# Low parts of two weight pieces by halves, low parts of probabilities in their usual place, both halves of one spectrum cast together

## The chip, the cores and the metric

The kernel runs on one core of a Trainium2 chip. It uses the core's engines side by side: TensorE for matmuls (PE in the profile, its weight loads PEld), VectorE (DVE), ScalarE (ACT), GpSimd (POOL), and SyncE (SP), which here only issues DMAs. Each engine works through its own queue in order; semaphores order the engines among each other. The metric is the time of one execution in device microseconds (us), as the median of several runs.

## The reference, cut to what matters

A trunk of two layers runs over a prompt of 2048 tokens and a sample of 512 tokens, 1024 channels wide, all in float32. Layer 0 is windowed attention, layer 1 Fourier mixing; each is gated, projected and added to its input.

```python
def attention_layer(x, g, w_in, w_out, sink, rel_bias):
    h = rmsnorm(x, g)
    z = h @ w_in                      # 1024 -> q 1024, k 256, v 256, gate 1024
    ...
    o = banded_gqa_with_sink(q, k, v, rel_bias, sink)   # 16 heads, 4 kv heads, |i-j| <= 128
    return x + (o * jax.nn.silu(gate)) @ w_out

def fourier_layer(x, g, w_gate, w_out):
    h = rmsnorm(x, g)
    hg = h.astype(jnp.float32).reshape(b, s, N_FGROUPS, FGROUP_CH)
    f = jnp.fft.fftn(hg, axes=(1, 3), norm="ortho").real
    gate = h @ w_gate
    return x + (f.reshape(b, s, d) * jax.nn.silu(gate)) @ w_out
...
    return rmsnorm(x, final_norm)
```

In the attention, each block of 128 queries meets three blocks of keys; scores get a bias, are exponentiated with their maximum (or the sink) taken off, divided by their sum, and multiplied with the values.

## The kernel before, in words

**Two parts for every operand.** A float32 operand of a matmul is split into a high part (a cast to the type `fp32r`, mostly on ACT) and a low part (the operand minus its high part, on DVE or POOL). A product is then three matmuls: high by high, high by low, low by high (`matmul3`, line 134, and `beside`, line 524).

**Chunks and periods.** The attention phase goes over five chunks of 512 tokens (`CHUNKS`); chunk 0 is the sample, chunks 1 to 4 the prompt. Within a chunk, 19 periods `n` are laid out. Two periods make a pair of heads `p`, one for each two of the chunk's four query blocks. A period also holds a quarter of the projections for the next heads (q and gate weights, tiles `wq`, `wg`, products in PSUM `pj`).

**The order in a period** is written out by hand: `FIRST` for chunk 0, `PERIOD` for the others, as pairs of a step's name and how many periods it lags. The steps that matter here, with their lines:

- `S1`, `S2`: scores on PE (line 661, into `spt`); `b..`: bias and maximum on DVE (line 680); `e..`: exponentials on ACT (line 688); `r..`: reciprocals on DVE (line 694); `m..`: division by the sum, on DVE (line 707 in chunk 0) or ACT (line 701).
- `T0`, `T1`: probabilities transposed on PE into `tp` (line 720); `hi0`, `hi1`: their high parts on ACT (line 733); `lo0`, `lo1`: their low parts on DVE (line 737), both into the tile `pts`.
- `AV1`, `AV2`: probabilities by values on PE (line 780, into `av`); `t2`, `add`: the two halves of that summed (ACT line 800, DVE line 810) into `o`; `mul`, `sp`, `lop`: gate (POOL line 816), high part (ACT line 821), low part (POOL line 825), into `uT`.
- `qH`, `qL`: the next heads' q split (ACT line 584, DVE line 585, tile `qab`), and beside them pieces of the keys (tile `kwin`; ACT line 398, DVE line 403). `W`, `WL`: the next weights split (ACT line 177, POOL line 182, four pieces of 256 columns) and stored to DRAM (POOL line 184) for the later chunks.
- `side`: in chunk 0 alone, at the end of periods 1 to 5, the late weight pieces.

`seq` chains the recorded order on PE, ACT and DVE. On POOL, `pieces` (line 962) is tied only to the last `lop`; the rest of POOL's order is what the scheduler makes of the operands.

**Late weight pieces.** The key weights (pieces 8 and 9, `LATE`) are used in chunk 0 before there is time to store their split form. So chunk 0 fetches each again later (`late_w`): `w32late` is loaded in period 1 or 3; in period 2 or 4 ACT casts the high part (`latehi`, line 1165), POOL forms the low part in four pieces of 256 columns (`latelo`, line 962), and POOL issues two DMAs that store both (line 1168). Line 1198 moves the step `lo1` ahead of `b2a` in periods 3 and 5 of chunk 0, the periods behind a late piece.

**Position transforms.** In the Fourier phase, `position` multiplies a spectrum, split by `halves_of` into high and low parts for each half of its 1024 columns (tile `gp`, ACT line 1713, DVE line 1714), with tables. `step` (line 1989) splits the first half of its first position ahead of time, and leaves the second half to `position`.

Of the kernel before, what the change touches and what calls it, by code (L numbers as in the profile page):

```python
# [14 lines left out]
ALU = mybir.AluOpType  # L15
# [17 lines left out]
LATE = (8, 9)  # L33
# [17 lines left out]
def f32(ap):  # L51
    return ap.bitcast(F32)
# [3 lines left out]
def encoder(  # L56
# [3 lines left out]
    PE, ACT, DVE, POOL, SP = nc.tensor, nc.scalar, nc.vector, nc.gpsimd, nc.sync  # L60
# [26 lines left out]
    wsd = [dram.tile([P, 2, D], F32R, name=f"wsd{i}") for i in range(28)]  # L87
# [50 lines left out]
    def fetch_w(n, name, late=None):  # L138

        w32 = stage[late is not None or n > 19 or n in (6, 7, 18, 19)](f"w32{name}")  # L140
        load = SP.dma_start(w32, w_in[n] if n < 20 else w_out[(n - 20) // 4, (n - 20) % 4])
        if late:
            after(load, late)
        last_fetch[0] = load
        return w32
# [44 lines left out]
    def after(ins, anchor):  # L190

        if anchor is not None:
            tc.add_manual_dep(ins.ins, anchor.ins.name, ISSUE, reason="issue order")
# [10 lines left out]
    def attention_phase():  # L204

        with ExitStack() as es:
# [750 lines left out]
            def pieces(out, a, b, op, n=2):  # L957

                for i in range(n):
                    cs = slice(i * 256, i * 256 + 256)  # L960

                    after(POOL.tensor_tensor(out[:, cs], a[:, cs], b[:, cs], op), last_lo[0])
# [129 lines left out]
            for c in range(len(CHUNKS)):  # L1092
# [67 lines left out]
                def late_w(i):  # L1160
                    w32 = fetch_w(LATE[i], f"late{i}", last_exp[0])

                    def split():
                        hi, lo = (xtile([P, D], F32R, f"late{part}{i}") for part in ("hi", "lo"))
                        seq(ACT, ACT.copy(hi, w32))
                        pieces(lo, w32, f32(hi), ALU.subtract, 4)
                        for part, t in enumerate((hi, lo)):
                            POOL.dma_start(f32(wsd[LATE[i]][:, part]), f32(t))

                    return split  # L1170

                def side(n):
                    if n in (1, 3):
                        side_steps.append(late_w(n // 2))
                    elif n in (2, 4):
                        side_steps.pop()()
                    if k_splits:
                        k_lows.append(k_splits.pop(0)())

                side_steps, k_lows = [], []  # L1180
                low_q, high_q, low_w = [], [], []
                for n in range(19):
# [12 lines left out]
                    order = [a for a in (PERIOD if c else FIRST) if n < 15 or a[0] not in ("hi0", "lo0")]  # L1195
                    if n == 1 and c:
                        order.sort(key=lambda a: a[0] == "qL")
                    if n in (3, 5) and not c:
                        low = order.index(("lo1", 1))
                        order.insert(order.index(("b2a", 0)), order.pop(low))  # L1200
                    if n >= 15:
                        for name, behind in (("hi0", ("T0",)), ("lo0", ("m2a", "m2b"))):
                            at_ = max(i for i, a in enumerate(order) if a[0] in behind)
# [47 lines left out]
    def fourier_phase(tail):  # L1251
        with ExitStack() as es:
# [300 lines left out]
            order = [[16, 17, 18, 19]] + [[a, a + 4, a + 8, a + 12] for a in range(4)]  # L1553
# [147 lines left out]
            def position_loads(name, tab, tiles):  # L1701
                return [gated(name, r, xtile) for r in tiles], table(name, tab, left)

            def halves_of(name, gr, gs, hf, after_one=None):

                out = []
                for i, g in enumerate((gr, gs)):
                    if i and after_one:
                        after_one()
                    if g is not None:  # L1710
                        t = main.tile([P, 2, 512], F32R, align_bytes=LINE, tag="hT", bufs=8, name=f"g{name}_{hf}_{i}")
                        gv = g[hf] if isinstance(g, list) else g[:, hf * 512 : hf * 512 + 512]
                        ACT.copy(t[:, 0], gv)
                        low = DVE.tensor_tensor(t[:, 1], gv, f32(t[:, 0]), ALU.subtract)
                        if chain.get("steps"):
                            seq("dve", low)
                        out.append(t)
                return out
# [98 lines left out]
            class Outs:  # L1817
# [53 lines left out]
                def rest(self):  # L1871
                    self.halve(3)
                    self.own(1, 1)
# [115 lines left out]
            def step(n, *positions):  # L1989
                new, held = [], []  # L1990
                for i, p in enumerate(positions):
                    held.append((position_loads(p[0], p[1], p[4]), None if i else [halves_of(p[0], p[2], p[3], 0), None]))

                def within():
                    for p, h in zip(positions, held):
                        new.extend(position(*p, *h))

                if not n:
                    within()
                end = finish(*pend.pop(0), None, within, n)  # L2000
                chain["turns"] = end
                new = turned(new)
                for f in pend:
                    finish(*f)
                pend[:] = new
# [82 lines left out]
            for i, l in enumerate((w0, w2)):  # L2088
                for a in range(3):
                    t = zt(f"ev{a}_{i}")  # L2090
# [34 lines left out]
            for a in range(4):  # L2125
                for i, l in enumerate((pc, qs)):
# [3 lines left out]
                    t = zt(f"od{a}_{i}")  # L2130
# [205 lines left out]
```

## Time and profile before

| | |
|---|---|
| median of 3 runs | 1536.61 us (1535.53 to 1537.4) |
| the profiled execution | 1536.59 us |
| its span in the profile | 1534.5 us |
| PE busy | 1519.9 us, 99% of the span |
| PE weight loads busy | 1340.0 us, 87% |
| DVE busy | 1119.7 us, 73% |
| ACT busy | 890.4 us, 58% |
| POOL busy | 453.1 us, 30% |
| low parts of the late pieces, L962 `latelo` | 8 instructions of 727 to 756 ns, 63.3 to 83.6 us after the start |
| casts of the spectrum at position 2, L1713 `gp<-g2r`, `g2s` | 4 instructions of 603 to 617 ns, 1355.2 to 1361.3 us after the start |

In rows of the timeline the first number is the start after the span's begin, the second the length, both in us; then engine, line, operation, output `<-` inputs, shapes, and how many instructions were merged into the row. In brackets stands how long the engine was idle before it, and what ended that. A DMA row of POOL is the issue, not the transfer. Records of matmuls overlap, since matmuls are pipelined.

### The profile page before, as it was taken

The numbers are of one execution on the slowest core, as the hardware profiler recorded it, in microseconds if no ns is written. First come the engines' busy times: TensorE is split into PE (matmuls) and PEld (weight loads), VectorE is DVE, ScalarE is ACT, GpSimd is POOL, SyncE is SP. The second block draws the span as 40 slices with busy tenths as digits, with TensorE's granted clock in tenths as the row PEclk, the third lists the DMA queues.
The fourth block names the chain that finished last, engine by engine and source line by source line (L and its number), as shares of the span: only waits on it lengthen the run. The fifth ranks groups of instructions, "written<-read, shape, count | busy, mean of one in ns | idle before, by whom it ended". The sixth has DMA issues, their size and how long they took to land.

```text
span 1534.5 us, 33665 instructions
## 1 busy us (share of the span) xinstructions
PE 1519.9 (99%) x13150; PEld 1340.0 (87%) x13150; DVE 1119.7 (73%) x2431; ACT 890.4 (58%) x1925; POOL 453.1 (30%) x616
## 2 busy tenths in 40 slices
PE   9999999999999999999999999999999999999998
PEld 7999889999898888999988899888888888888886
DVE  5898665777638776468764577667888878888896
ACT  6788634787237884268862577646655654343343
POOL 2576652422414323315124142222212111011100
PEclk9999999999999999999999999999999999999999
DMA  8687687685857766867649666584657679557852
GB/s 322 224 301 247 232 335 280 220 301 174 321 192 244 242 222 231 304 211 228 227 166 379 231 214 233 207 299 163 240 206 249 210 243 413 174 180 278 299 182 91
DMA packets 100731, 372.71 MB, mean 243 GB/s; under 512 B 11236, under 2 KB 22252, under 8 KB 83421
## 3 DMA queue, kind: packets, MB, share of 16 engines
q1 hardware_dynamic: 82716, 297.38, 56.1%
q0 software_dynamic: 16688, 70.04, 11.7%
q10 hardware_dynamic: 1168, 3.15, 0.6%
q8 instruction: 103, 1.69, 0.4%
q14 instruction: 56, 0.45, 0.1%
HBM read 280.06 MB, written 90.47 MB: 241 GB/s over the span
## 4 chain that ended last, share of the span: by engine, by line
PE 88%; DVE 7%; issue 2%; ACT 2%; DMA 1%; POOL 0%; POOLq 0%; ACTq 0%; DVEq 0%; SPq 0%
PE pj L524 27%; PE W L134 6%; PE pj L134 6%; PE tp L134 5%; PE av L780 5%; PE spt L661 5%; PE av L134 5%; PE spt L134 4%; PE tp L720 3%; PE Wo L134 3%; PE Z L134 3%; PE fo L134 2%; PE z L1420 2%; PE Zo L134 2%; PE X L134 2%
## 5 line engine op out<-in xcount | busy, mean ns | idle before, releaser
L524 PE MATMUL pj<-h,wg 64*128 64x512 f32 x1920 | 437.7, 389 | 0.0
L524 PE MATMUL pj<-h,wq 64*128 64x512 f32 x1560 | 379.1, 389 | 0.0
L524 PEld LDWEIGHTS pj<-h,wg 64*128 64x128 f32 x1920 | 332.2, 185 | 17.7
L524 PEld LDWEIGHTS pj<-h,wq 64*128 64x128 f32 x1560 | 285.0, 185 | 12.7 <-DVE q L580 0.2
L680 DVE CUSTOM_DVE_ANT_0 S<-spt,b 128x385 f32<-128x385 f32 (+1 forms) x320 | 165.0, 525 | 80.1 <-PE spt L661 77.5
L688 ACT ACTIVATE S<-S 128x385 f32<-128x385 f32 (+1 forms) x320 | 189.1, 592 | 56.5 <-DVE S L680 37.0
L733 ACT CAST pts<-tp 128x768 fp32r<-128x768 f32 (+1 forms) x160 | 121.3, 758 | 76.2 <-PE av L780 43.0
L737 DVE TENSOR_TENSOR pts<-tp,pts 128x768 fp32r<-128x768 f32 (+1 forms) x160 | 144.1, 901 | 13.1 <-ACT pts L733 12.8
L825 POOL TENSOR_TENSOR uT<-o,uT 128x256 fp32r<-128x256 f32 x75 | 56.9, 759 | 228.3 <-ACT uT L821 228.0
L661 PE MATMUL spt<-kwin,qab 64*128 64x384 f32 (+1 forms) x960 | 121.0, 340 | 0.9 <-DVE S L680 0.7
L780 PE MATMUL av<-pts,v 64*128 64x256 f32 (+3 forms) x1680 | 121.3, 263 | 0.5 <-DVE pts L737 0.4
L134 PE MATMUL fo<-wo,tTu 128*128 128x512 f32 x480 | 113.7, 392 | 0.0
L780 PEld LDWEIGHTS av<-pts,v 64*128 64x128 f32 (+1 forms) x1680 | 106.4, 159 | 4.4 <-DVE pts L737 1.1
L134 PEld LDWEIGHTS fo<-wo,tTu 128*128 128x128 f32 x480 | 88.7, 188 | 18.0
L720 PEld LDWEIGHTS tp<-ident,S 64*128 64x128 f32 x1792 | 89.1, 138 | 11.0 <-DVE pts L737 2.8
L720 PE MATMUL tp<-ident,S 64*128 64x64 f32 x1792 | 92.5, 223 | 1.9 <-DVE S L707 1.7
L816 POOL TENSOR_TENSOR o<-o,s 128x256 f32<-128x256 f32 x75 | 55.7, 743 | 112.3 <-DVE o L810 87.9
L661 PEld LDWEIGHTS spt<-kwin,qab 64*128 64x128 f32 x960 | 82.9, 187 | 3.7 <-issue 1.8
L703 DVE TENSOR_SCALAR S<-S 128x384 f32<-128x384 f32 (+1 forms) x192 | 84.0, 466 | 0.3
L279 DVE SCALAR_TENSOR_TENSOR h<-xk,g0s,h 128x512 fp32r<-128x512 f32 x40 | 46.7, 1179 | 48.5 <-ACT h L278 48.3
L524 PE MATMUL pj<-wo,uT 64*128 64x512 f32 x360 | 74.7, 391 | 0.0
L278 ACT ACTIVATE h<-xk,g0s 128x512 fp32r<-128x512 f32 x40 | 28.7, 724 | 74.1 <-POOL xk L274 73.3
(379 smaller groups left out, 3359.8 us busy)
## 6 DMA issues: line engine op xcount, KB each, us to landing
wo<-wsd SPq DMA_DIRECT2D x32, 1024.0 KB, 6.3
wq<-wsd SPq DMA_DIRECT2D x31, 1024.0 KB, 6.6
wg<-wsd SPq DMA_DIRECT2D x31, 1024.0 KB, 6.2
x<-x1d SPq DMA_DIRECT2D x40, 512.0 KB, 4.0
b<-b21d SPq DMA_DIRECT2D x40, 512.0 KB, 5.0
b<-rowd SPq DMA_DIRECT2D x40, 384.0 KB, 4.2
xs<-in_x_dram SPq DMA_DIRECT2D x23, 512.0 KB, 6.6
s2d<-gt POOLq DMA_DIRECT2D x40, 256.0 KB, 4.0
```

The lines of the kernel that those rows point to most:

```text
L134: ins = pe(PE.matmul(out, a[i], b[j], start=start and i + j == 0, stop=stop and i == 1, skip_group_check=more))
L524: out.last[h] = pe(PE.matmul(out.ps, a[i], b[j], **out.flags()))
L661: pe(PE.matmul(spt[j][:, 2 + k0 * P : 2 + k1 * P], res["q"][rows, qp, b * P : (b + 1) * P], kwin[g][rows, kp, b * P + k0 * P : b * P + k1 ...
L680: seq(DVE, DVE.tensor_tensor_reduce(out=s[:, e0:e1], in0=ps[:, 1 + e0 : 1 + e1], in1=st["bias"][:, j, 386 - e1 : 386 - e0][:, ::-1], scale ...
L688: last_exp[0] = seq(ACT, ACT.activation(s[:, e0:e1], s[:, e0:e1], AF.Exp, bias=s[:, 386:387], scale=-1.0, accum_out=s[:, 387:388]))
L703: seq(DVE, DVE.tensor_scalar(s[:, ks], s[:, ks], den, None, ALU.mult))
L720: pe(PE.transpose(ps[h][:, kb, j, :], s[rows, j, 1 + kb * P : 1 + (kb + 1) * P], ident[rows, rows]))
L733: seq(ACT, ACT.copy(hi, ps))
L737: seq(DVE, DVE.tensor_tensor(lo, ps, f32(hi), ALU.subtract))
L780: last[i][h] = pe(PE.matmul(to, v, pt, start=not swap and n == 0, stop=swap and n == len(todo[h]) - 1, skip_group_check=True,))
L816: eng.tensor_tensor(o, o, s, ALU.mult)
L825: low = eng.tensor_tensor(lo, o, f32(hi), ALU.subtract)
```

## The change

Three edits, two of them in chunk 0 of the attention and one in the Fourier phase.

```diff
                     def split():
                         hi, lo = (xtile([P, D], F32R, f"late{part}{i}") for part in ("hi", "lo"))
                         seq(ACT, ACT.copy(hi, w32))
-                        pieces(lo, w32, f32(hi), ALU.subtract, 4)
-                        for part, t in enumerate((hi, lo)):
-                            POOL.dma_start(f32(wsd[LATE[i]][:, part]), f32(t))
+                        halves = [[t[:, cs] for t in (lo, w32, f32(hi))] for cs in (slice(0, 512), slice(512, 1024))]
+                        pieces(*halves[0], ALU.subtract)
+                        POOL.dma_start(f32(wsd[LATE[i]][:, 0]), f32(hi))
+
+                        def rest():
+                            pieces(*halves[1], ALU.subtract)
+                            POOL.dma_start(f32(wsd[LATE[i]][:, 1]), f32(lo))
+
+                        return rest
 
                     return split
 
                 def side(n):
                     if n in (1, 3):
                         side_steps.append(late_w(n // 2))
-                    elif n in (2, 4):
-                        side_steps.pop()()
+                    if n in (2, 3, 4, 5):
+                        rest = side_steps.pop(0)()
+                        if rest:
+                            side_steps.insert(0, rest)
...
                     if n == 1 and c:
                         order.sort(key=lambda a: a[0] == "qL")
-                    if n in (3, 5) and not c:
-                        low = order.index(("lo1", 1))
-                        order.insert(order.index(("b2a", 0)), order.pop(low))
...
-                    held.append((position_loads(p[0], p[1], p[4]), None if i else [halves_of(p[0], p[2], p[3], 0), None]))
+                    held.append((
+                        position_loads(p[0], p[1], p[4]),
+                        None if i else [halves_of(p[0], p[2], p[3], hf) if hf == 0 or n == 3 else None for hf in range(2)],
+                    ))
```

`pieces` without a last argument makes two pieces of 256 columns. So each late piece's low part is formed as two pieces and a store of the high part at the end of one period (2 or 4), and two pieces and a store of the low part at the end of the next (3 or 5).

On POOL, in chunk 0 behind the low parts of gate weight 2 (`wg_2`), stood this before, around the first late piece:

```order
L182 TENSOR_TENSOR wg_2_883<-w32g_2_622,wg_2_883 128x256 x4
L184 DMA wsd_108<-wg_2_883 128x2048
L962 TENSOR_TENSOR latelo_892<-w32late_739,latehi_891 128x256 x4
L1168 DMA wsd_102<-latehi_891 128x1024
L1168 DMA wsd_102<-latelo_892 128x1024
L825 TENSOR_TENSOR uT_0_481<-o_0_0_844,uT_0_481 128x256
L816 TENSOR_TENSOR o_0_2_1000<-o_0_2_1000,s_0_758 128x256
```

and now, on POOL at the same place:

```order
L182 TENSOR_TENSOR wg_2_883<-w32g_2_622,wg_2_883 128x256 x4
L184 DMA wsd_108<-wg_2_883 128x2048
L962 TENSOR_TENSOR latelo_892<-w32late_739,latehi_891 128x256 x2
L1168 DMA wsd_102<-latehi_891 128x1024
L825 TENSOR_TENSOR uT_0_481<-o_0_0_844,uT_0_481 128x256
L962 TENSOR_TENSOR latelo_892<-w32late_739,latehi_891 128x256 x2
L1172 DMA wsd_102<-latelo_892 128x1024
L816 TENSOR_TENSOR o_0_2_997<-o_0_2_997,s_0_758 128x256
```

The second two pieces and their store have moved behind one `uT`, and stand ahead of the next period's `o` (line 816) and weights, though they are written at that period's end. The second late piece, behind `wg_3`, reads the same.

On DVE, in period 3 of chunk 0, behind the next heads' q (`qab`), stood this before; `ISA` of line 680 is the bias and maximum of the scores, each with a row that reads its accumulator:

```order
L585 TENSOR_TENSOR qab_2_979<-q_2_913,qab_2_979 128x512
L403 TENSOR_TENSOR kwin<-kt_1_455,kwin 64x512
L694 RECIPROCAL S_1_3_977<-S_1_3_977 128x2
L810 TENSOR_TENSOR o_0_2_1000<-av,t_0_2_949 64x256 x2
L737 TENSOR_TENSOR pts_1_0_916<-tp,pts_1_0_916 128x2x6x64
L680 ISA S_1_2_1037<-spt_74,b_1_542 128x385
L680 ISA S_1_2_1037 128x1
L680 ISA S_1_2_1037<-spt_75,b_1_542 128x385
L680 ISA S_1_2_1037 128x1
L707 TENSOR_SCALAR S_1_3_977<-S_1_3_977 128x256
```

and now, on DVE at the same place:

```order
L585 TENSOR_TENSOR qab_2_976<-q_2_910,qab_2_976 128x512
L403 TENSOR_TENSOR kwin<-kt_1_455,kwin 64x512
L694 RECIPROCAL S_1_3_974<-S_1_3_974 128x2
L810 TENSOR_TENSOR o_0_2_997<-av,t_0_2_946 64x256 x2
L680 ISA S_1_2_1033<-spt_74,b_1_542 128x385
L680 ISA S_1_2_1033 128x1
L680 ISA S_1_2_1033<-spt_75,b_1_542 128x385
L680 ISA S_1_2_1033 128x1
L737 TENSOR_TENSOR pts_1_0_913<-tp,pts_1_0_913 128x2x6x64
L707 TENSOR_SCALAR S_1_3_974<-S_1_3_974 128x256
```

The low parts of the probabilities (line 737) have moved behind the two scores of line 680. Period 5 reads the same.

The third edit has `step` record the casts of position 2's second half (`gp<-g2r`, `gp<-g2s`) next to those of the first. On all five engines the built order of instructions around them is the same with it as before; apart from the two places above, no engine's order differs.

## The prediction

> **What bounds the kernel now.** I read the page first: the span, and the chain of work that ended last, by engine.
>
> ```profile
> span 1534.5 us, 33665 instructions
> ...
> PE 88%; DVE 7%; issue 2%; ACT 2%; DMA 1%; POOL 0%; POOLq 0%; ACTq 0%; DVEq 0%; SPq 0%
> ```
>
> TensorE (PE) sets the end. An edit on VectorE (DVE) or GpSimd (POOL) counts only where PE stands still for it. So next came PE's list of waits over the whole span (total us, times, longest); these are its two largest.
>
> ```profile
> PE tp L720 <- DVE S L707: 1.7, 2, 0.9
> PE ABp L134 <- DVE gp L1714: 1.2, 3, 0.5
> ```
>
> The first is two waits in chunk 0, the second belongs to the position transforms of the Fourier phase. No DMA stands in that list, so a shift of PE in chunk 0 is taken up by nothing later and reaches the end. Busy time by stretch finds the two waits (stretch, its length, then busy us and count for PE, PEld, DVE, ACT, POOL).
>
> ```profile
> 60.00:80.00 20.00, 18.96 (x234) 18.00 (x232) 18.73 (x51) 16.88 (x39) 15.86 (x24) 1.00 0.68 246
> 80.00:100.00 20.00, 18.95 (x223) 17.68 (x221) 19.01 (x55) 16.89 (x39) 15.45 (x23) 1.00 0.76 294
> 100.00:120.00 20.00, 20.00 (x242) 19.39 (x242) 17.23 (x54) 17.56 (x43) 11.23 (x16) 1.00 0.82 286
> ```
>
> PE loses about 1.04 us in each of the first two stretches and nothing in the third, and DVE is nearly full where PE loses. The clock is granted in full (1.00). PE's timeline shows the loss: `av` L780 is AV1, `tp` L720 behind it T0.
>
> ```profile
> 68.75 0.70 PE L780 MATMUL av<-pts,v 64*128 64x256 f32 x7
> 69.65 0.51 PE L780 MATMUL av<-pts,v 64*64 64x256 f32 x3 [0.19 <-DVE pts L737]
> 71.00 0.46 PE L720 MATMUL tp<-ident,S 64*128 64x64 f32 x8 [0.84 <-DVE S L707]
> ...
> 78.58 0.51 PE L780 MATMUL av<-pts,v 64*128 64x256 f32 x5
> ...
> 105.16 0.63 PE L780 MATMUL av<-pts,v 64*128 64x256 f32 x7
> ...
> 113.49 0.69 PE L780 MATMUL av<-pts,v 64*128 64x256 f32 x8
> ```
>
> From one AV1 to the next PE takes 78.58 - 68.75 = 9.83 us here and 113.49 - 105.16 = 8.33 us in the same kind of period later. So a late piece costs **1.5 us**, part of it hidden in overlapping matmul records, and the two pieces **3.0 us**: that is all there is to win, 0.2% of the time.
>
> Why DVE is late stands in its own timeline and in POOL's.
>
> ```profile
> 63.66 0.69 DVE L737 TENSOR_TENSOR pts<-tp,pts 128x512 fp32r<-128x512 f32 x1 [0.37 <-ACT pts L733]
> 64.27 2.36 DVE L585 TENSOR_TENSOR qab<-q,qab 128x512 fp32r<-128x512 f32 x1
> 66.56 1.22 DVE L403 TENSOR_TENSOR kwin<-kt,kwin 64x512 fp32r<-64x512 f32 x1
> 67.70 0.15 DVE L694 RECIPROCAL S<-S 128x2 f32<-128x2 f32 x1
> 67.78 0.83 DVE L810 TENSOR_TENSOR o<-av,t 64x256 f32<-64x256 f32 x2
> 68.64 0.96 DVE L737 TENSOR_TENSOR pts<-tp,pts 128x768 fp32r<-128x768 f32 x1
> ...
> 70.46 0.47 DVE L707 TENSOR_SCALAR_CACHE_REDUCE S<-S 128x256 f32<-128x256 f32 x1
> ```
>
> ```profile
> 62.65 0.58 POOL L184 DMA_DIRECT2D wsd<-wg  x1 [0.30 <-POOL wg L182]
> 63.25 2.82 POOL L962 TENSOR_TENSOR latelo<-w32late,latehi 128x256 fp32r<-128x256 f32 x4
> 66.02 0.57 POOL L1168 DMA_DIRECT2D wsd<-latehi  x1
> 66.58 0.54 POOL L1168 DMA_DIRECT2D wsd<-latelo  x1
> 67.14 1.24 POOL L825 TENSOR_TENSOR uT<-o,uT 128x256 fp32r<-128x256 f32 x1
> ```
>
> L585 and L403 have both operands in SBUF. Their groups (ns min/median/max) and the second late piece's two rows say what they cost alone and here:
>
> ```profile
> L585 DVE TENSOR_TENSOR qab<-q,qab x8: 679/682/2359, 37.0 to 150.2; 128x512 fp32r<-128x512 f32 x8
> L403 DVE TENSOR_TENSOR kwin<-kt,kwin x8: 683/689/1220, 29.7 to 93.5; 64x512 fp32r<-64x512 f32 x8
> ```
>
> ```profile
> 82.72 2.17 DVE L585 TENSOR_TENSOR qab<-q,qab 128x512 fp32r<-128x512 f32 x1
> 84.91 1.13 DVE L403 TENSOR_TENSOR kwin<-kt,kwin 64x512 fp32r<-64x512 f32 x1
> ```
>
> L737 reads PSUM and took 0.69 us beside L962. L585 was held until the fourth piece ended at 66.07 and finished 0.56 us later, at 66.63; it passed two piece ends (the pieces start every 0.69 us) without getting in. L403 then finished 0.66 us behind the second L1168. Behind L403 DVE has no gap until L707 releases T0: from L403's end, 67.78, to T0, 71.00, are **3.22 us** of DVE work.
>
> **The change, part by part.**
>
> *Late pieces by halves.* On paper the stream of four L962 becomes two streams in two periods. In the built order the second half and its DMA stand right behind one `uT` L825, ahead of the next period's work. POOL's line becomes: two L962, the first L1168, L825, two L962, the second store; none of the middle ones waits for anything but POOL's own order. From 63.25: two pieces at 0.69 to 64.63; L1168 0.57 to 65.20; L825 from 65.22; two pieces from 65.9 to 67.33. For L825 alone I take this row, with DVE out of its way:
>
> ```profile
> 73.12 0.75 POOL L825 TENSOR_TENSOR uT<-o,uT 128x256 fp32r<-128x256 f32 x1
> ```
>
> The work is the same, in one block without a pause; only the longest run of equal pieces is halved.
>
> What that does to L585 hangs on whether DVE gets in where one POOL instruction ends and the next is ready. No row shows a stream with a DMA inside. The nearest are two streams of four L274 against L279, which also has both operands in SBUF. The first has no POOL DMA ahead of it:
>
> ```profile
> 801.22 6.16 POOL L274 TENSOR_TENSOR xk<-xk,invb 128x512 f32<-128x512 f32 x4 [5.47 <-ACT invb L247]
> 803.51 1.01 DVE L279 SCALAR_TENSOR_TENSOR h<-xk,g0s,h 128x512 fp32r<-128x512 f32 x1 [1.94 <-ACT h L278]
> ```
>
> The second follows a DMA issue on POOL at once:
>
> ```profile
> 820.74 0.55 POOL L907 DMA_DIRECT2D xr<-in_x_dram  x1 [0.35 <-DMA xk<-in_xT_dram]
> 821.30 5.04 POOL L274 TENSOR_TENSOR xk<-xk,invb 128x512 f32<-128x512 f32 x4
> 823.40 3.50 DVE L279 SCALAR_TENSOR_TENSOR h<-xk,g0s,h 128x512 fp32r<-128x512 f32 x1 [11.84 <-ACT h L278]
> ```
>
> In the first, L279 is through at 804.52, in the middle of a stream that ends at 807.38. In the second it ends at 826.90, after the whole stream (826.34). The late pieces are of the second kind: L184 ends at 63.23, the stream starts at 63.25, and L585 waited for all of it, both times. I take this as the rule here: **a POOL stream that starts right behind a DMA issue does not let a two-operand DVE instruction in until it has run dry**. Before the change it ran dry at 66.07, because the second L1168 waits for the pieces. Now nothing in the line waits until 67.33. So L585 is held to 67.33 and ends at 67.33 + 0.56 = 67.89 (1.26 later), L403 follows at its median, 0.69, and ends about 68.50 instead of 67.78: **+0.72 us**. Bounds: if L585 goes at 64.63 and L403 right behind it, L403 ends at 65.9 and the whole 1.5 us is won; if L403 also waits for the second store as it did before (start 67.33 + 0.30, 0.54 long, then 0.65), it ends at 68.82, +1.04. I take +0.72, as L403 is then alone with a DMA issue that no ready stream follows.
>
> The Trainium skill, page "SBUF — State Buffer", section "Who interferes with whom", says that a VectorE instruction with two SBUF inputs and a GpSimd instruction that reads SBUF exclude each other, and that whichever starts first holds the shared ports for that one instruction. By it L585 would have been in at the end of the piece it met, near 64.7; the trace, with 2.36 us, disagrees. What the rule would make of the change is the second rival.
>
> *The low parts back in place.* L737 (0.96 us) at 68.64 goes behind the two L680 of the next scores (69.51 to 70.5). Both orders do the same work before L707, so T0's release doesn't move: cost nothing, hidden by DVE's own queue. AV1's last products wait for L737 about 0.95 us longer, until just before L707; they take 0.51 us (the row at 69.65) and L707 0.47, so they lie beside it. That cover is thin: without it each piece costs about 0.1 us more.
>
> *Both halves of a spectrum cast together.* The order of all five engines is the same around the casts of position 2; the edit changes when they are recorded, and the scheduler had already put them there. The wait on L1714 (1.2 us in three times) is its ceiling; I take nothing.
>
> **The sum.** The profiled execution took 1536.59 us, 2.1 over its span, and the median of three is 1536.61, so it stands for them. Two pieces at +0.72 make +1.44: **1538.0 us**. With the bound of +1.04 it is 1538.7.
>
> **Rivals.**
>
> *DVE gets in beside the first store (faster).* L585 did end just beside the first L1168 before (66.63 against 66.59). If a DMA issue opens the line whatever stands behind it, L585 ends at 64.69 + 0.56 = 65.25. If L403 follows at once, it ends at 65.9, T0 comes at its undisturbed place and the full 3.0 us are won: 1533.6. Against it: in the old order L403 lost that place to POOL's next instruction both times.
>
> *One instruction at a time (faster).* L585 goes at 64.69, L403 loses to L825 and goes at its end, 65.97, ending at 66.6; T0 at 66.6 + 3.22 = 69.8, 1.2 earlier, twice: 1534.2. For it stands L279 at 803.51, against it L279 at 823.40 and L585. It is what the Trainium skill's rule, cited above, would give.
>
> *L585 goes, L403 doesn't.* L403 meets L825 and the two pieces as one stream and ends at 67.33 + 0.65 = 67.98, +0.20 twice: 1537.0. For it stands L403's 1.22 and 1.13 us.
>
> *L403 behind the second store too (slower).* As worked out, 1538.7; decided by whether that DMA issue holds L403 when no ready instruction follows it.
>
> *The change doesn't do what it says.* Its third part does not, and the second half isn't a period later; both are in the sum.
>
> **Chances.** Forecast 0.38, with L403 behind the store too 0.14, L403 alone held 0.20, one at a time 0.13, everything won 0.10, something else 0.05. The three times spread from 1535.53 to 1537.4, 0.9 us to a side, so the range is 1534.0 to 1539.2: it takes in the first three cases, and about half of one at a time. About 0.2% (3.1 us) is what a measurement of this kernel can tell from no change. All that could be won is 3.0 us, so faster by more than that gets 0.08, from the case that wins everything and a little of one at a time; slower 0.04, from the store case with a push of the spread; no change 0.88.
>
> **What would show it.** Right: L585 after the change near 3.6 us in both places (64.27 to 67.9), L403 near 0.7, PE's idle time in AV1 and before T0 together near 1.75 us instead of 0.19 + 0.84, AV1 to AV1 near 10.55 instead of 9.83. Wrong: L585 near 1.0, so a DMA issue lets DVE in; then L403's length tells the rivals apart: 0.7 (all won), 1.4 (one at a time), 2.7 (held by the rest). For the moved L737, PE's wait should move from before T0 into AV1. For the third part, the casts of `gp` from `g2r` and `g2s` should stand in the same order. A difference in any stage after chunk 0 that is more than a shift would make the whole account wrong.

## The result, and the profile after

| | before | after |
|---|---|---|
| median of 18 runs each, same chip | 1536.85 us (1535.53 to 1539.98) | 1534.29 us (1533.6 to 1537.94) |
| ratio | | 0.9983, 95% interval 0.9976 to 0.999 |
| the profiled execution | 1536.59 us | 1535.48 us |
| its span | 1534.5 us | 1533.7 us |

The kernel is 2.6 us faster; forecast was 1.4 us slower. The two profiled executions are only 1.1 us apart, because chunk 0 began later in the one after (its first late piece starts at 64.78 us, before at 63.25), so the stage is compared by lengths within it. First, busy time by stretch of the kernel after (columns as in the prediction), then the two entries of PE's list of waits that answer to those of before.

```profile
60.00:80.00 20.00, 19.66 (x239) 19.07 (x237) 19.08 (x54) 18.00 (x42) 16.54 (x24) 1.00 0.77 277
80.00:100.00 20.00, 19.43 (x233) 18.54 (x231) 19.32 (x57) 17.72 (x39) 16.43 (x24) 1.00 0.88 319
100.00:120.00 20.00, 20.00 (x242) 19.60 (x241) 17.32 (x54) 17.56 (x43) 10.85 (x16) 1.00 0.80 282
```

```profile
PE av L780 <- DVE pts L737: 0.9, 2, 0.5
...
PE ABp L134 <- DVE gp L1719: 0.7, 2, 0.3
```

PE stands still for 0.34 and 0.57 us in the first two stretches, not for 1.04 and 1.05. Its wait has moved from before T0 (`tp` L720, released by L707) into AV1 (`av` L780, released by L737). PE's timeline after, AV1 and then the next AV1, for the first late piece and then the second:

```profile
70.05 0.63 PE L780 MATMUL av<-pts,v 64*128 64x256 f32 x7
71.02 0.51 PE L780 MATMUL av<-pts,v 64*64 64x256 f32 x3 [0.34 <-DVE pts L737]
...
79.01 0.85 PE L780 MATMUL av<-pts,v 64*128 64x256 f32 x10
...
87.18 0.65 PE L780 MATMUL av<-pts,v 64*128 64x256 f32 x7
88.35 0.50 PE L780 MATMUL av<-pts,v 64*64 64x256 f32 x3 [0.52 <-DVE pts L737]
...
96.35 1.11 PE L780 MATMUL av<-pts,v 64*128 64x256 f32 x10
```

AV1 to AV1 is now 79.01 - 70.05 = **8.96** and 96.35 - 87.18 = **9.17 us**, against 9.83 and 9.84 before (the second from the starts of its matmuls, as in the table of runs below). Why stands in DVE's and POOL's timelines after, at the first late piece:

```profile
65.19 0.69 DVE L737 TENSOR_TENSOR pts<-tp,pts 128x512 fp32r<-128x512 f32 x1 [0.38 <-ACT pts L733]
65.80 1.24 DVE L585 TENSOR_TENSOR qab<-q,qab 128x512 fp32r<-128x512 f32 x1
66.96 1.22 DVE L403 TENSOR_TENSOR kwin<-kt,kwin 64x512 fp32r<-64x512 f32 x1
...
70.01 0.95 DVE L737 TENSOR_TENSOR pts<-tp,pts 128x768 fp32r<-128x768 f32 x1
70.88 0.47 DVE L707 TENSOR_SCALAR_CACHE_REDUCE S<-S 128x256 f32<-128x256 f32 x1
```

```profile
64.16 0.59 POOL L184 DMA_DIRECT2D wsd<-wg  x1 [0.30 <-POOL wg L182]
64.78 1.45 POOL L962 TENSOR_TENSOR latelo<-w32late,latehi 128x256 fp32r<-128x256 f32 x2
66.17 0.57 POOL L1168 DMA_DIRECT2D wsd<-latehi  x1
66.76 0.88 POOL L825 TENSOR_TENSOR uT<-o,uT 128x256 fp32r<-128x256 f32 x1
67.61 1.87 POOL L962 TENSOR_TENSOR latelo<-w32late,latehi 128x256 fp32r<-128x256 f32 x2
```

L585 does not wait until GpSimd's line, its ready instructions one behind another, has run dry. It ends at 67.04, 0.81 us behind the second piece's end (64.78 + 1.45 = 66.23), while the first store is being issued. In turn it holds up `uT`: 0.88 us instead of 0.75. L403 then waits for that `uT` only, and ends 0.54 us behind it, at 68.18; the third piece pays for that (two pieces take 1.87 us, not 1.45). From the first piece's start to L403's end it is 68.18 - 64.78 = 3.40 us, where it was 67.78 - 63.25 = 4.53. The second late piece reads the same, DVE and POOL:

```profile
83.15 1.11 DVE L585 TENSOR_TENSOR qab<-q,qab 128x512 fp32r<-128x512 f32 x1
84.27 1.13 DVE L403 TENSOR_TENSOR kwin<-kt,kwin 64x512 fp32r<-64x512 f32 x1
```

```profile
81.97 1.44 POOL L962 TENSOR_TENSOR latelo<-w32late,latehi 128x256 fp32r<-128x256 f32 x2
83.36 0.57 POOL L1168 DMA_DIRECT2D wsd<-latehi  x1
83.95 0.90 POOL L825 TENSOR_TENSOR uT<-o,uT 128x256 fp32r<-128x256 f32 x1
```

These are the places of the rival *one instruction at a time*. Its time was 1534.2; that the median came so close to it is in part luck, since neither AV1 to AV1 nor the stage below fell by as much as it had worked out.

The change also made a new meeting. L596 works on the tiles `th` and `s`, both in SBUF, and took 0.68 us in the periods behind both late pieces before. Behind the second one it now starts while L184 is being issued (91.39 to 91.99) and ends 0.56 us behind the `uT` that follows (92.00 to 92.75):

```profile
91.77 1.54 DVE L596 SCALAR_TENSOR_TENSOR s<-th,s 128x512 f32<-128x512 f32 x1
```

### The profile page after: what moved, and what is told of

Its sections match the earlier page's. It is cut to its first block, busy times and chain, and to the rows that moved or that the text cites. A ratio compares the mean times of both kernels' runs of the same rounds, so it can differ in the third digit from the quotient of the medians.

```text
span 1533.7 us, 33665 instructions
## 1 busy us (share of the span) xinstructions
PE 1520.7 (99%) x13150; PEld 1351.5 (88%) x13150; DVE 1119.0 (73%) x2431; ACT 890.3 (58%) x1925; POOL 453.1 (30%) x616
## 4 chain that ended last, share of the span: by engine, by line
PE 88%; DVE 7%; issue 2%; ACT 2%; DMA 1%; POOL 0%; POOLq 0%; DVEq 0%; SPq 0%; ACTq 0%
PE pj L524 27%; PE W L134 6%; PE pj L134 6%; PE av L780 6%; PE tp L134 5%; PE spt L661 5%; PE av L134 5%; PE spt L134 4%; PE tp L720 3%; PE Wo L134 3%; PE Z L134 3%; PE fo L134 2%; PE z L1425 2%; PE Zo L134 2%; PE X L134 2%
## 5 line engine op out<-in xcount | busy, mean ns | idle before, releaser
L737 DVE TENSOR_TENSOR pts<-tp,pts 128x768 fp32r<-128x768 f32 (+1 forms) x160 | 144.0, 900 | 11.9 <-ACT pts L733 11.4
L780 PE MATMUL av<-pts,v 64*128 64x256 f32 (+3 forms) x1680 | 122.2, 262 | 1.0 <-DVE pts L737 0.9
L780 PEld LDWEIGHTS av<-pts,v 64*128 64x128 f32 (+1 forms) x1680 | 108.3, 159 | 3.4 <-DVE pts L737 1.6
L720 PEld LDWEIGHTS tp<-ident,S 64*128 64x128 f32 x1792 | 90.4, 138 | 8.0 <-DVE pts L737 2.6
L720 PE MATMUL tp<-ident,S 64*128 64x64 f32 x1792 | 93.3, 223 | 0.1
L816 POOL TENSOR_TENSOR o<-o,s 128x256 f32<-128x256 f32 x75 | 55.7, 743 | 109.6 <-DVE o L810 86.2
L279 DVE SCALAR_TENSOR_TENSOR h<-xk,g0s,h 128x512 fp32r<-128x512 f32 x40 | 46.9, 1185 | 51.1 <-ACT h L278 51.1
```

Of the source, the lines that this page charges most:

```text
L720: pe(PE.transpose(ps[h][:, kb, j, :], s[rows, j, 1 + kb * P : 1 + (kb + 1) * P], ident[rows, rows]))
L737: seq(DVE, DVE.tensor_tensor(lo, ps, f32(hi), ALU.subtract))
L780: last[i][h] = pe(PE.matmul(to, v, pt, start=not swap and n == 0, stop=swap and n == len(todo[h]) - 1, skip_group_check=True,))
L816: eng.tensor_tensor(o, o, s, ALU.mult)
```

## The experiments

Two things had to be told apart: which of the three edits carries the gain, and why L585 got in although a DMA issue stands right ahead of the line. In the table, "L585" and "L403" are their lengths beside the first and the second late piece; "AV1" is AV1 to AV1 in these two periods; "stage" is the time from the AV1 ahead of all this (61.8 us after the start in the profile after) to the one seven distances later, from the starts of the matmuls in each run's trace. Undisturbed distances are 8.2 to 8.35. "L585", "L403", "AV1" and "stage" come from one profiled execution of each run, the medians from all of its executions.

| run | median, us | before beside it | ratio, 95% interval | L585 | L403 | AV1 | stage |
|---|---|---|---|---|---|---|---|
| before | 1536.85 | | | 2.36, 2.17 | 1.22, 1.13 | 9.83, 9.84 | 61.38 |
| the change | 1534.29 | 1536.85 | 0.9983 (0.9976 to 0.999) | 1.24, 1.11 | 1.22, 1.13 | 8.96, 9.17 | 59.62 |
| halves alone | 1534.49 | 1537.08 | 0.9984 (0.9975 to 0.9993) | 1.24, 1.12 | 1.21, 1.13 | 8.93, 9.00 | 60.0 |
| low parts back alone | 1536.2 | 1537.08 | 0.9998 (0.9989 to 1.0007) | 2.34, 2.17 | | 9.84, 9.83 | 61.37 |
| casts alone | 1536.91 | 1537.08 | 0.9997 (0.9988 to 1.0006) | 2.34, 2.19 | | 9.85, 9.84 | 61.42 |
| no store between | 1537.6 | 1536.57 | 1.0009 (1.0 to 1.0019) | 3.05, 2.88 | 0.67, 0.68 | 9.86, 9.85 | 61.83 |
| store behind | 1534.0 | 1536.57 | 0.9986 (0.9977 to 0.9996) | 0.72, 0.96 | 1.22, 0.68 | 8.42, 8.70 | 59.5 |
| uT ahead | 1538.38 | 1536.39 | 1.0008 (0.9999 to 1.0018) | 3.05, 2.90 | 0.67, 0.68 | 9.85, 11.41 | 63.45 |
| store between four | 1534.01 | 1536.39 | 0.9982 (0.9972 to 0.9991) | 1.25, 1.11 | 1.22, 1.13 | 8.97, 9.00 | 59.24 |
| behind the keys | 1535.82 | 1537.08 | 0.9994 (0.9985 to 1.0003) | 0.68, 1.07 | 0.68, 0.68 | 8.33, 8.83 | 60.3 |
| the same, later norms | 1533.55 | 1536.39 | 0.9977 (0.9968 to 0.9986) | 0.68, 1.05 | 0.68, 0.68 | 8.33, 8.83 | 58.55 |
| the change again | 1534.47 | 1536.39 | 0.998 (0.9971 to 0.999) | 1.25, 1.11 | 1.22, 1.13 | 8.94, 9.12 | 59.66 |

### Which edit carries it

**Halves alone**: the change with the other two edits undone (lines that begin with `-` are the change's).

```diff
+                    if n in (3, 5) and not c:
+                        low = order.index(("lo1", 1))
+                        order.insert(order.index(("b2a", 0)), order.pop(low))
...
-                    held.append((
-                        position_loads(p[0], p[1], p[4]),
-                        None if i else [halves_of(p[0], p[2], p[3], hf) if hf == 0 or n == 3 else None for hf in range(2)],
-                    ))
+                    held.append((position_loads(p[0], p[1], p[4]), None if i else [halves_of(p[0], p[2], p[3], 0), None]))
```

> The halves alone, with the low parts of probabilities still ahead of the next scores. Theory A (the halves carry the whole gain: the first store between the halves lets L585 in early, and between L403's end and T0 the same DVE work stands in either order): as the change, near 1534.3 us, ratio 0.998; L585 near 1.2 and 1.1 us, L403 near 1.2 and 1.1, AV1 to AV1 in the two late periods near 9.0 and 9.2 us instead of 9.83; PE waits before T0, not in AV1. Theory B (part of the gain is the order of the low parts): at least 0.7 us of the 2.6 missing, 1535 or more, with AV1 to AV1 at 9.4 or more.

**Low parts back alone** is the kernel before without its line 1198 and the two lines under it, and nothing else of the change:

```diff
-                    if n in (3, 5) and not c:
-                        low = order.index(("lo1", 1))
-                        order.insert(order.index(("b2a", 0)), order.pop(low))
```

> The low parts of probabilities back in place alone, late pieces in one stream of four as before. Theory A: as before, ratio 1.000 within 0.1%; L585 2.2 to 2.4 us, AV1 to AV1 9.8 us in the two late periods, the idle time of PE moved from before T0 into AV1. Theory B: faster by 0.7 us or more, with AV1 to AV1 near 9.4.

**Casts alone** is the kernel before with the third edit of the change:

```diff
-                    held.append((position_loads(p[0], p[1], p[4]), None if i else [halves_of(p[0], p[2], p[3], 0), None]))
+                    held.append((
+                        position_loads(p[0], p[1], p[4]),
+                        None if i else [halves_of(p[0], p[2], p[3], hf) if hf == 0 or n == 3 else None for hf in range(2)],
+                    ))
```

> The casts of position 2 recorded together, alone. The built order is that of before on every engine. Theory A (no effect): ratio 1.000, whatever differs is the spread of runs, and the casts of g2r and g2s stand as far apart as before. Theory B (it changes waits or buffers): more than 0.1% either way, with another wait at ABp in the profile around 1355 to 1365 us.

The halves alone give 1534.49, the whole change 1534.29; the other two lie at 0.9998 and 0.9997 with 1 well inside their intervals. The halves carry all that can be measured in the time. The stage is 0.37 us shorter in the change than in *halves alone* (59.62 and 60.0), so the low parts may add a little beside the halves; the medians can't show it.

### What the line behind a DMA issue does

**No store between**: the change, but the store of the high part is issued behind the second half, so that two pieces, `uT` and two pieces follow L184 with no DMA among them.

```diff
                         pieces(*halves[0], ALU.subtract)
-                        POOL.dma_start(f32(wsd[LATE[i]][:, 0]), f32(hi))
 
                         def rest():
                             pieces(*halves[1], ALU.subtract)
+                            POOL.dma_start(f32(wsd[LATE[i]][:, 0]), f32(hi))
                             POOL.dma_start(f32(wsd[LATE[i]][:, 1]), f32(lo))
```

> The change, with the first store moved behind the second half, so that GpSimd's line is a DMA issue, two pieces, uT, two pieces, and then both stores. Theory A (a GpSimd stream behind a DMA issue lets a VectorE instruction with two SBUF operands in only when it has run dry; in the change it was the store in the middle that opened it): L585 held over all five instructions, near 3.0 us, L403 then free or held by the stores; AV1 to AV1 10 us or more in the late periods; 1 us or more slower than before. Theory B (VectorE gets in at the end of any GpSimd instruction): L585 near 1.0, L403 near 1.2, as fast as the change or faster.

POOL's timeline of this run, then DVE's:

```profile
62.36 0.58 POOL L184 DMA_DIRECT2D wsd<-wg  x1 [0.30 <-POOL wg L182]
62.96 1.44 POOL L962 TENSOR_TENSOR latelo<-w32late,latehi 128x256 fp32r<-128x256 f32 x2
64.36 0.72 POOL L825 TENSOR_TENSOR uT<-o,uT 128x256 fp32r<-128x256 f32 x1
65.05 1.42 POOL L962 TENSOR_TENSOR latelo<-w32late,latehi 128x256 fp32r<-128x256 f32 x2
```

```profile
63.98 3.05 DVE L585 TENSOR_TENSOR qab<-q,qab 128x512 fp32r<-128x512 f32 x1
66.95 0.67 DVE L403 TENSOR_TENSOR kwin<-kt,kwin 64x512 fp32r<-64x512 f32 x1
```

L585 passes three ends of instructions (the second piece, `uT`, the third piece) and ends 0.56 us behind the last piece (66.47). All the difference from the change is the place of one DMA issue. The time, 1.0 us above before with an interval that begins at 1.0, can't be told from before.

**Store behind**: the kernel before, with the store of the gate weight (L184) behind the late pieces and their stores, so that no DMA issue stands ahead of them.

```diff
-                POOL.dma_start(f32(wsd[n]), f32(w))
+                store = POOL.dma_start(f32(wsd[n]), f32(w))
+                if n in (14, 15):
+                    after(store, late_low[0])
...
                         pieces(lo, w32, f32(hi), ALU.subtract, 4)
                         for part, t in enumerate((hi, lo)):
-                            POOL.dma_start(f32(wsd[LATE[i]][:, part]), f32(t))
+                            late_low[0] = POOL.dma_start(f32(wsd[LATE[i]][:, part]), f32(t))
```

> The kernel of before, with the store of gate weight 2 (and 3) moved behind the late piece's stores: the stream of four pieces has no DMA issue ahead of it, and uT stands ahead of it. Theory A (only a stream right behind a DMA issue holds VectorE until it has run dry): L585 gets in at the end of a piece, 0.7 to 1.3 us, L403 at the end of a later one, the pieces then take 0.4 us longer each time; AV1 to AV1 near 9.0, near the change's time. Theory B (any stream of ready GpSimd instructions holds it): L585 1.8 to 2.4 us, AV1 to AV1 9.5 or more, time as before.

POOL and DVE of this run (lines of DVE are two higher: L587 is L585, L405 is L403):

```profile
62.12 0.74 POOL L827 TENSOR_TENSOR uT<-o,uT 128x256 fp32r<-128x256 f32 x1
62.82 3.73 POOL L964 TENSOR_TENSOR latelo<-w32late,latehi 128x256 fp32r<-128x256 f32 x4
```

```profile
64.08 0.72 DVE L587 TENSOR_TENSOR qab<-q,qab 128x512 fp32r<-128x512 f32 x1
64.73 1.22 DVE L405 TENSOR_TENSOR kwin<-kt,kwin 64x512 fp32r<-64x512 f32 x1
```

Both are through at 65.95, while the pieces run on to 66.55. The pieces give way instead: four take 3.73 us, in the prediction's POOL timeline 2.82. The same stream, of the same instructions, lets DVE in at the end of each instruction when no DMA issue stands ahead of it. Only the first late piece shows this: at the second, L585 met the last piece alone (0.96 us). The stage, 59.5, is not as short as the two AV1 to AV1 (8.42 and 8.70) would make it, because the distance between them is 9.38; ahead of it L596 met a `uT` behind L184 and took 1.30 us, though no run tests whether that is the reason. This run also put `uT` ahead of the pieces, hence the next.

**uT ahead**: the kernel before with that `uT` moved ahead of the four pieces; L184 stays right ahead of it.

```diff
-                        pieces(lo, w32, f32(hi), ALU.subtract, 4)
-                        for part, t in enumerate((hi, lo)):
-                            POOL.dma_start(f32(wsd[LATE[i]][:, part]), f32(t))
+
+                        def low():
+                            pieces(lo, w32, f32(hi), ALU.subtract, 4)
+                            for part, t in enumerate((hi, lo)):
+                                POOL.dma_start(f32(wsd[LATE[i]][:, part]), f32(t))
+
+                        whole.append(low)
...
+                            if name == "lop" and whole:
+                                whole.pop()()
```

> The kernel before, with the uT (L825) that stood behind the late pieces moved ahead of all four of them; the store of the gate weight (L184) still stands right ahead of that uT. POOL: four L182, L184, L825, four L962, two stores. The run with the store behind the pieces had taken that DMA issue away and put uT ahead as well; this one keeps the DMA issue. Theory A (it is the DMA issue right ahead that keeps DVE out until the line has run dry): L585 takes 2.4 us or more in both places, to the end of the fourth piece, AV1 to AV1 9.8 or more, time 1536 to 1538. Theory B (uT's place alone brought the gain): L585 0.7 to 1.3, AV1 to AV1 8.4 to 9.0, time near 1534.

DVE and POOL of this run, and one stretch of its busy times (clock third from the end):

```profile
65.94 3.05 DVE L585 TENSOR_TENSOR qab<-q,qab 128x512 fp32r<-128x512 f32 x1
```

```profile
64.32 0.58 POOL L184 DMA_DIRECT2D wsd<-wg  x1 [0.30 <-POOL wg L182]
64.92 0.75 POOL L825 TENSOR_TENSOR uT<-o,uT 128x256 fp32r<-128x256 f32 x1
65.62 2.82 POOL L962 TENSOR_TENSOR latelo<-w32late,latehi 128x256 fp32r<-128x256 f32 x4
```

```profile
90.00:100.00 10.00, 9.03 (x88) 8.83 (x90) 8.64 (x28) 7.48 (x18) 4.94 (x8) 0.83 0.78 265
```

With `uT` in the place of the run before but the DMA issue ahead, L585 ends at 68.99, 0.55 us behind the fourth piece: it is the DMA issue, not `uT`. The time can't be told from before (the interval begins at 0.9999). The 11.41 us of the second AV1 to AV1 are not this wait alone: the granted clock was 0.83 in that stretch of the profiled execution, so neither they nor this run's stage are used.

**Store between four**: the kernel before, all in one period as there; the edit only issues the store of the high part between the second and the third piece. In the built order the store of the low part then also stands behind `uT`, not ahead of it.

```diff
-                        pieces(lo, w32, f32(hi), ALU.subtract, 4)
                         for part, t in enumerate((hi, lo)):
+                            cs = slice(512 * part, 512 * part + 512)
+                            pieces(lo[:, cs], w32[:, cs], f32(hi[:, cs]), ALU.subtract)
                             POOL.dma_start(f32(wsd[LATE[i]][:, part]), f32(t))
```

> The kernel before, with all pieces in one period as there, but the store of the high part issued between the second and the third piece. POOL: four L182, L184, two L962, store, two L962, uT L825, store. Theory A (a DMA issue inside a line lets DVE in, and once DVE has held the line up it yields at the end of each instruction): L585 1.1 to 1.3 us, ending 0.8 us behind the second piece; the third piece 1.1 to 1.2 instead of 0.69; L403 0.9 to 1.3, in at the end of the third piece; AV1 to AV1 8.9 to 9.2; time 1534 to 1535. Theory B (it opens the line only while the DMA issue lasts; the two pieces and uT behind it are again a stream behind a DMA issue): L585 the same, L403 2.3 us or more, until uT's end; AV1 to AV1 9.8 or more; time as before, 1536 to 1537.5. Theory C (what opened the line in the change was uT standing there, not the DMA issue): L585 2.3 us or more as before.

POOL and DVE of this run:

```profile
62.73 0.59 POOL L184 DMA_DIRECT2D wsd<-wg  x1 [0.30 <-POOL wg L182]
63.34 1.45 POOL L962 TENSOR_TENSOR latelo<-w32late,latehi 128x256 fp32r<-128x256 f32 x2
64.72 0.57 POOL L1169 DMA_DIRECT2D wsd<-latehi  x1
65.32 2.03 POOL L962 TENSOR_TENSOR latelo<-w32late,latehi 128x256 fp32r<-128x256 f32 x2
67.31 0.72 POOL L825 TENSOR_TENSOR uT<-o,uT 128x256 fp32r<-128x256 f32 x1
67.99 0.57 POOL L1169 DMA_DIRECT2D wsd<-latelo  x1
```

```profile
64.35 1.25 DVE L585 TENSOR_TENSOR qab<-q,qab 128x512 fp32r<-128x512 f32 x1
65.53 1.22 DVE L403 TENSOR_TENSOR kwin<-kt,kwin 64x512 fp32r<-64x512 f32 x1
```

L585 ends at 65.60, 0.81 us behind the second piece (64.79), as in the change. L403 gets in at the end of the third piece, though two more ready instructions follow that piece. The third piece had itself been held up by L585 (0.87 us, two take 2.03), and I read it so that the line stays open once that has happened; no run varies this alone. The second store comes at 67.99, when L585 and L403 are long through, so its place can't be what let them in. The time is that of the change. So moving one DMA issue from behind the third and fourth piece to ahead of them is enough for the gain; neither the second period nor `uT` between the halves is needed. Whether it must be a DMA issue, or any 0.57 us without a piece would do, no run here separates.

### Whether the two waits are all there is

**Behind the keys**: the change, but the four halves lie in periods 3 to 6, each half's pieces wait for the keys' low part (L403) of their period, and the gate of `o` (L816) waits for the last half's store. So POOL doesn't meet L403 at all and L585 only through other work. (The diff is against the kernel before; the change's other two edits are in this run too.)

```diff
-                        pieces(lo, w32, f32(hi), ALU.subtract, 4)
-                        for part, t in enumerate((hi, lo)):
-                            POOL.dma_start(f32(wsd[LATE[i]][:, part]), f32(t))
+                        def half(part, t):
+                            for j in range(2):
+                                cs = slice(512 * part + 256 * j, 512 * part + 256 * j + 256)
+                                ins = POOL.tensor_tensor(lo[:, cs], w32[:, cs], f32(hi[:, cs]), ALU.subtract)
+                                if j == 0:
+                                    after(ins, last_lo[0])
+                                    tc.add_manual_dep(ins.ins, last_key[0].ins.name, DONE, reason="behind the keys")
...
+                            last_half[0] = POOL.dma_start(f32(wsd[LATE[i]][:, part]), f32(t))
...
+                        halves.extend((lambda: half(0, hi), lambda: half(1, lo)))
```

> The late pieces by halves, each half made to wait for the low part of the keys (L403) of its period, so that no GpSimd stream of theirs meets L585 or L403; the four halves lie in periods 3 to 6. Theory A (all of the loss is L585 and L403 held by these streams): L585 near 0.68 us, L403 near 0.69 us in all periods, AV1 to AV1 8.2 to 8.4 us throughout, and 1.3 to 1.7 us less than the change, near 1532.8 to 1533. Theory B (GpSimd has no room for a half behind L403: the gate of o, L816, comes later, and with it the next weights and stores): L585 and L403 free, but AV1 to AV1 stays near 9.0 in some periods, time as the change or more.

Both AV1 to AV1 fall to 8.33 and 8.83, but the next one is 10.31, and the time, 1535.82, can't be told from before. What took the gain back stands in the timelines of ACT and PE:

```profile
97.18 1.06 ACT L223 ACTIVATE xs<-xs 128x1024 f32<-128x1024 f32 x1 [2.19 <-DMA xs<-in_x_dram]
```

```profile
100.32 0.58 PE L720 MATMUL tp<-ident,S 64*128 64x64 f32 x12 [1.43 <-DVE pts L737]
```

ACT's L223, a square for the norm of chunk 1, stands in ACT's queue ahead of the exponentials and waits 2.19 us for the load of its tile; PE then waits 1.43 us for probabilities. Theory B expected a loss of that size at another place (POOL's `mul`), so it was right in the time only. To see whether that wait is all, the statistics of that norm begin one period later:

```diff
-                        if i == 24:
+                        if i == (24 if c else 28):
```

> As the run with the half pieces behind the keys, but the statistics of chunk 1's norm begin one period later (position 28 instead of 24), so that ACT's L223 no longer stands in its queue for an x tile that was loaded late. Theory A (that wait was what the run with the pieces behind the keys gave back): AV1 to AV1 8.2 to 8.4 us in all periods, perhaps 8.8 once where uT meets the second L585; no wait of ACT for a DMA at 95 to 97 us; about 1.4 us under that run and 0.7 to 1.2 us under the change, near 1533.3 us. Theory B (the late x tile stops something else, its transpose or its copies, whatever position it is read at): one AV1 to AV1 of 9 us or more in one of the next periods, time as the change or above it.

Busy time by stretch and DVE's timeline of this run:

```profile
60.00:80.00 20.00, 20.00 (x249) 19.63 (x248) 18.88 (x56) 18.32 (x42) 15.30 (x23) 1.00 0.75 288
80.00:100.00 20.00, 19.80 (x231) 18.98 (x230) 19.13 (x56) 17.29 (x40) 15.97 (x25) 1.00 0.71 237
```

```profile
65.86 0.68 DVE L585 TENSOR_TENSOR qab<-q,qab 128x512 fp32r<-128x512 f32 x1
66.45 0.68 DVE L403 TENSOR_TENSOR kwin<-kt,kwin 64x512 fp32r<-64x512 f32 x1
```

PE is full in the first stretch and stands still for 0.2 us in the second. The stage takes 58.55 us instead of 61.38, 2.83 less, and the median is 1536.39 - 1533.55 = 2.84 us under before. Theory A held but for the distance behind the second late piece, 8.47. The median is 0.92 us under the change beside it, which was run once more for this comparison:

> The change itself, beside the others on the same chip. Both theories: 1534 to 1535, L585 1.24 and 1.11 us, L403 1.22 and 1.13. It is there for the comparison with the run with later norm statistics.

The stage is shorter here (58.55 against 59.66), but the two intervals overlap (0.9968 to 0.9986 and 0.9971 to 0.999), so it is not settled that this version beats the change.

## Why the prediction was wrong

- **What bounds the kernel**: right. PE sets the end, and a late piece costs 1.5 us: with L585 and L403 both free, AV1 to AV1 fell from 9.83 to 8.33. That a shift reaches the end fits too: in the six runs whose interval lies below 1 the stage is 1.4 to 2.8 us shorter than before's and the median 1.9 to 2.8 lower. It is not measured more finely than that. The change's stage is 1.76 us shorter and its median 2.6 lower, with an interval of about 1.5 to 3.7; that 2.83 and 2.84 agree in the last run is luck.
- **The failed step** is the sentence "I take this as the rule here: a POOL stream that starts right behind a DMA issue does not let a two-operand DVE instruction in until it has run dry", as it was put to use: "Now nothing in the line waits until 67.33. So L585 is held to 67.33". The rule as such held for L585 in two runs. For the line with its first store taken out, the prediction's own working gives an L585 of 67.89 - 0.57 - 64.27 = 3.05 us, and *no store between* measured 3.05; *uT ahead* did as well; and without a DMA ahead (*store behind*) it took 0.72. What failed was to count the store inside the line as one more instruction of the stream. It opens the line: L585 1.24 and 1.11 us, where 3.6 was forecast, and L403 ended 3.40 us behind the stream's start, not 68.50 - 63.25 = 5.25. *Store between four* shows it with one edit from before. The direction was wrong for this reason; the range, 1534.0 to 1539.2, took the measured 1534.29 in only at its lower edge.
- The evidence was read and put aside. Before, the prediction let the line run dry at the first store, "because the second L1168 waits for the pieces"; its own rows show no such wait (66.02 + 0.57 = 66.59, and the second store starts at 66.58). So nothing in them set the first store before apart from the one in the change. The prediction saw L585 end beside the first L1168 before, and argued against the rival from L403, which "lost that place to POOL's next instruction". But "No row shows a stream with a DMA inside" was also said, and the case that no row shows was then given the rule's answer with the largest single chance, and the two rivals in which L585 and L403 both come early 0.23 together.
- **L403**: forecast 0.69, measured 1.22 and 1.13. The step behind it, that it is free beside a DMA issue "that no ready stream follows", is right where it applies (0.67 and 0.68 in *no store between* and in *uT ahead*, beside the stores). In the change it applies nowhere, since L585 is early and L403 meets `uT`.
- **The size**: the rival *one instruction at a time* had L403 through at 66.6 for a stream from 63.25, so 3.35 us behind its start; it was 3.40. On DVE that is 1.13 us per piece (4.53 to 3.40), near its 1.2. At AV1 it came out as 0.87 (9.83 to 8.96) and 0.67 (9.84 to 9.17). Over the stage it is 1.76: the distances ahead of the two fell (8.44 and 8.54 before, 8.25 and 8.17 after), and the one behind the second rose from 8.20 to 8.53. This rise of 0.33 goes with L596 held for 1.54 us (in *store between four* L596 takes 0.81 there and the distance is 8.22), but no run tests whether the one makes the other. Twice 1.2 is 2.4; the medians differ by 2.6.
- **The low parts back in place**: right, nothing. PE's wait did move into AV1, as forecast: 0.9 us in two, where *halves alone* keeps 0.9 us in two before T0.
- **The casts**: right, nothing. The wait `ABp` on `gp` fell from 1.2 us in three to 0.7 in two in the profile after, but was 1.2 in three again in the change's second profile.
- **The Trainium skill's rule** (page "SBUF — State Buffer", section "Who interferes with whom"), that such a pair excludes one another for one instruction at a time, was set aside for the trace of before. It describes the change, *store between four* and *store behind*, in the first two but for the 0.25 us named below. It does not describe before (2.36), *no store between* (3.05) or *uT ahead* (3.05), where several instructions ended and L585 didn't get in.

## What to carry to other kernels

Where two engines keep each other out, look at what stands right ahead of the stream that wins, and not only at its length: behind a DMA issue on GpSimd the same four pieces kept VectorE out to their end, and with a DMA issue among them, or none ahead, they let it in. So try issuing a store as soon as its data is ready, between the pieces of a long stream, and not all stores behind it, and then look for meetings that the moved work makes elsewhere. And when a forecast rests on a place that no row shows, keep the outcomes on both sides of it at chances that admit this, however good the rule from the neighbouring rows looks.

## What the hardware showed that was not expected

- A DMA issue on GpSimd had two effects on L585, a VectorE instruction with both operands in SBUF, at both late pieces of all nine runs in which the pieces stand behind L184 and meet it. Right ahead of a stream it closed the line until the stream ended (2.17 to 3.05 us); inside the stream it opened it (1.1 to 1.25), and after that the line yielded at the end of each instruction, though a DMA issue stood right ahead of the rest too (L403 in *store between four*). What in GpSimd does this is not in the trace.
- The closing is not without exception. Two L274 right behind the store L171 kept L279 out to the end of the second in ten of the twelve profiles, and let it in at the end of the first in two, *casts alone* and *store behind*. Before, then *casts alone*, whose built order is the same:

```profile
199.56 3.43 DVE L279 SCALAR_TENSOR_TENSOR h<-xk,g0s,h 128x512 fp32r<-128x512 f32 x1 [8.63 <-ACT h L278]
```

```profile
199.12 3.58 POOL L274 TENSOR_TENSOR xk<-xk,invb 128x640 f32<-128x640 f32 x2
199.35 1.91 DVE L279 SCALAR_TENSOR_TENSOR h<-xk,g0s,h 128x512 fp32r<-128x512 f32 x1 [8.63 <-ACT h L278]
```

So something besides the order decides as well; what it is stays open.
- L585 ended 0.81 us behind the second piece in the change, where a store and then `uT` follow, but 0.56 us behind the last piece in before and in *no store between*, where two stores follow. These 0.25 us are not explained.
- An instruction that waits this way is logged as running, so no list of waits shows it; only its length against its group's median does (2.36 against 0.68).
